# A hybrid RWKV backbone on one core: the RWKV stage, its group norms, the conditioning and the filters put in an order by a list scheduler for all five engines, and the triangular inverse made by 16-blocks on GpSimd

## The chip, the cores and the metric

The kernel runs on one core of a Trainium2 chip. The metric is the device time of one execution in microseconds (us); the kernel before was timed three times. Engines are named as in the profile: PE is TensorE (PEld its weight loads), DVE VectorE, ACT ScalarE, POOL GpSimd, SP SyncE, which here issues the DMA transfers and computes nothing.

## The reference

Two layers over 1024 latent and 256 context tokens of width 1024, in fp32. Layer 0 has retention and RWKV-7 side by side, layer 1 a Hyena long convolution and neighbourhood attention. The change touches RWKV (8 heads of 64, both directions), its group norm and bonus, the conditioning, and the Hyena filters:

```python
shift, scale, gate = jnp.split(sc @ ada_w[i] + ada_b[i], 3, axis=-1)   # sc = silu(c); the same with silu(c_ctx)
...
for d in range(2):
    w_log = -jax.nn.softplus(-(w0[d] + jnp.tanh(wd[:, :, d]) @ w2[d])) - 0.5
    a = jax.nn.sigmoid(a0[d] + ad[:, :, d] @ a2[d])
...
def step(s, inp):                                    # rwkv7_scan, one token
    r_t, w_t, k_t, v_t, kk_t, a_t = inp
    sa = jnp.einsum('bhvk,bhk->bhv', s, -kk_t)
    s = s * w_t[:, :, None, :] + sa[..., None] * (kk_t * a_t)[:, :, None, :] + v_t[..., None] * k_t[:, :, None, :]
    return s, jnp.einsum('bhvk,bhk->bhv', s, r_t)
...
gn = ((rw_y - mean) * lax.rsqrt(var + RWKV_GN_EPS)).reshape(bl, l, RWKV_W) * rw_ln_w + rw_ln_b
bonus = sum(jnp.sum(r * dirs[d][1] * rw_rk, axis=-1, keepdims=True) * v for d in range(2))
rw_o = (gn + bonus.reshape(bl, l, RWKV_W)) * jax.nn.silu(u[..., E_WZ:E_SHIFT])
...
hid = jnp.sin(f2 * (jnp.sin(f1 * (z @ w1 + b1)) @ w2 + b2))             # hyena_filters
h = (hid @ w3).reshape(length, HY_ORDER, 2, HY_W)
```

## The kernel before

The program runs in phases. Phase A makes layer 0's projections and the retention; its last projection product starts on PE at 673 us, and the rest of the retention follows. Phase B, which the change rewrites, is the RWKV stage with all that runs beside it. Phase C multiplies by layer 0's output weights; the later phases are layer 1.

RWKV is computed in chunks of 64 tokens, two chunks to a group, ten groups, both directions d side by side on the two halves of the 128 partitions. For each group and direction, `half` handles two head pairs at a time: loads `kkr`; the low-rank products `lora` on PE and four tanh `tw` on ACT; a running sum `cum` on DVE; decays `Pt`, `Pi` on ACT; scaled keys `AR`, `BK` on DVE and POOL; their transposes `BT`. `stage1` then makes the scores `sc` on PE, which DVE takes out of PSUM under a mask in two parts: `Ga` (key against key, to be inverted) and `Gr` (read-out). `inverse` inverts I minus 32 strictly triangular 64x64 matrices per group. It writes their diagonal 32-blocks to DRAM (`la`), loads them back with one matrix row to a free index (`AL`), does 31 steps of a multiply (L956) and an add (L958) on DVE, and goes back through DRAM (`lt`, `TT`). `merge` makes the off-diagonal block out of three rounds of 32x32 products on PE (`t11p`, `xp`, `t21p`), each copied out by ACT and DVE. `recur` walks the two chunks: read-out `rp` (from the state `SP`, with `Ga` and later `Gr`), `up` (the inverse times the right-hand side `RH`), the state update `sp`, and the result `Yg`, which goes to DRAM as `y`.

Beside it run three other pieces of work. `ada_gate` and `ada_cols` make the rest of the conditioning in 32 blocks of 128 columns, each a load of 512 KB (`aw`) and eight products (`adaps`) whose stationary side is only 2 columns wide. `RwkvOut.block` makes norm, bonus and gate for 128 tokens at a time, 10 blocks, as soon as both directions have them. `hyena_kernels` makes the filters (`hkps`, `HK`, `EO`, `d1ps`, `d2t`, `d2ps`), begun in the last groups and finished in phase C. The order on each engine comes from the tile framework, which schedules what the program emits; recurrence and group preparation are emitted under `tc.high_priority`, the side work by `next(side)` between the steps of `phase_b`.

## Time and profile before

| | before |
|---|---|
| median of 3 runs | 2403.91 us (2401.15 to 2409.35) |
| the profiled execution | 2408.1 us, span 2406.3 us |
| mean granted TensorE clock | 0.941 of full speed |
| PE busy in the span | 2206.3 us (92%) |
| DVE, ACT, POOL busy | 1213.9, 930.2, 791.6 us |
| instructions | 44212 |

Read it so: the share of 92% is an average over phases with different limits. What counts for this change are the rows from 680 to 1400 us, where PE is less busy and its granted clock lower than elsewhere.

### The profile page before, as it was taken

The page shows a single profiled execution, that of the slowest core. Times are in us where ns is not written, and L with a number is a line of the kernel's source. Part 1 is how long each engine was busy: PE and PEld are TensorE (multiplying, and loading weights), DVE is VectorE, ACT ScalarE, POOL GpSimd, SP SyncE. Part 2 cuts the span into 40 slices and gives each one's busy share as a digit, 9 for nine tenths or more (in the row PEclk, how much of TensorE's full clock was granted, in tenths as well). Part 3 has the DMA queues.
Part 4 walks back from the last instruction along what each step waited for, and adds up shares of the span by engine and source line. Part 5 has one row for each costly group of instructions (what it writes and reads, how often), then busy time and mean ns, then how long its engine had stood idle before and what let it go on. Part 6 is the DMA issues. An engine that isn't in the chain of part 4 may idle for free. (4 is left out here: it accounts for less than half of the span.)

```text
span 2406.3 us, 44212 instructions
## 1 busy us (share of the span) xinstructions
PE 2206.3 (92%) x16800; PEld 1854.7 (77%) x16800; DVE 1213.9 (50%) x3043; ACT 930.2 (39%) x1996; POOL 791.6 (33%) x1040
## 2 busy tenths in 40 slices
PE   7999999999989788898868899999979999989997
PEld 3778878777856677777766689889968888878987
DVE  6301222234347687777777756610036666634438
ACT  4321124445345354444335543321124444444432
POOL 2313625453556243333214534521111011010133
PEclk9999999999988787788889999999989999999999
DMA  7323333544276544455455443433276462175453
GB/s 245 95 78 106 116 115 123 155 126 136 91 211 180 119 124 126 108 134 138 101 145 170 151 160 107 148 115 109 75 184 162 130 169 93 53 242 156 132 161 123
DMA packets 398365, 325.66 MB, mean 135 GB/s; under 512 B 135038, under 2 KB 337928, under 8 KB 397898
## 3 DMA queue, kind: packets, MB, share of 16 engines
q1 hardware_dynamic: 398154, 322.85, 46.5%
q8 instruction: 133, 2.18, 0.4%
q14 instruction: 78, 0.64, 0.1%
HBM read 227.58 MB, written 95.17 MB: 134 GB/s over the span
## 5 line engine op out<-in xcount | busy, mean ns | idle before, releaser
L386 POOL TENSOR_TENSOR wlo<-wraw,whi 128x512 fp32r<-128x512 f32 (+1 forms) x60 | 81.6, 1380 | 354.7 <-ACT whi L385 303.0
L418 PE MATMUL dps<-n1hi,whi 128*128 128x512 f32 x448 | 187.5, 418 | 0.1
L418 PE MATMUL dps<-n1hi,wlo 128*128 128x512 f32 x448 | 177.4, 396 | 0.0
L418 PE MATMUL dps<-n1lo,whi 128*128 128x512 f32 x448 | 177.1, 395 | 0.0
L418 PE MATMUL dnp<-wlo,nhi 128*128 128x512 f32 x400 | 159.1, 399 | 2.9 <-POOL wlo L402 2.9
L418 PE MATMUL dnp<-whi,nlo 128*128 128x512 f32 x400 | 158.3, 397 | 0.0
L418 PE MATMUL dnp<-whi,nhi 128*128 128x512 f32 x400 | 153.3, 399 | 1.6 <-ACT whi L401 1.6
L402 POOL TENSOR_TENSOR wlo<-wraw,whi 128x512 fp32r<-128x512 f32 (+1 forms) x72 | 92.3, 1291 | 131.4 <-ACT whi L401 126.5
L418 PE MATMUL mmps<-nhi,whi 128*128 128x512 f32 (+1 forms) x336 | 123.4, 368 | 2.9 <-ACT vto L533 2.1
L327 PE MATMUL adaps<-aw,sc 128*2 128x128 f32 (+1 forms) x640 | 114.2, 335 | 11.6 <-DMA aw<-in_ada_w 9.6
L418 PE MATMUL mmps<-nlo,whi 128*128 128x512 f32 (+1 forms) x336 | 120.8, 361 | 0.0
L418 PE MATMUL mmps<-nhi,wlo 128*128 128x512 f32 (+1 forms) x336 | 119.6, 365 | 0.0
L956 DVE TENSOR_TENSOR tm<-RR,AL 128x126 f32<-128x126 f32 (+22 forms) x310 | 99.7, 322 | 19.5 <-DMA AL<-la 13.3
L1254 POOL TENSOR_TENSOR hn<-hn,xr 128x256 f32<-128x256 f32 x60 | 47.2, 791 | 175.4 <-DVE hn L1253 158.8
L418 PEld LDWEIGHTS dps<-n1hi,wlo 128*128 128x128 f32 x448 | 85.1, 190 | 18.6
L327 PEld LDWEIGHTS adaps<-aw,sc 128*2 128x2 f32 x640 | 55.3, 94 | 56.4 <-issue 16.7
L958 DVE TENSOR_TENSOR RR<-RR,tm 128x126 f32<-128x126 f32 (+22 forms) x310 | 94.6, 305 | 6.2
L418 PE MATMUL ops<-whi,clo 128*128 128x256 f32 x320 | 89.7, 287 | 6.1 <-DVE clo L1187 6.1
L418 PEld LDWEIGHTS dps<-n1hi,whi 128*128 128x128 f32 x448 | 85.9, 192 | 11.0 <-ACT whi L385 0.6
L418 PEld LDWEIGHTS dps<-n1lo,whi 128*128 128x128 f32 x448 | 85.6, 191 | 10.5
L418 PE MATMUL ops<-whi,chi 128*128 128x256 f32 x320 | 92.8, 292 | 0.0
L418 PEld LDWEIGHTS dnp<-wlo,nhi 128*128 128x128 f32 x400 | 75.7, 189 | 22.0 <-POOL wlo L402 4.7
(400 smaller groups left out, 6188.9 us busy)
## 6 DMA issues: line engine op xcount, KB each, us to landing
aw<-in_ada_w SPq DMA_DIRECT2D x32, 512.0 KB
kkr<-kkr SPq DMA_DIRECT2D x40, 384.0 KB
wraw<-in_odd_w_in SPq DMA_DIRECT2D x56, 256.0 KB
wraw<-in_even_w_in SPq DMA_DIRECT2D x48, 256.0 KB
bi<-in_nab SPq DMA_DIRECT2D x64, 192.0 KB
aw<-in_ada_w SPq DMA_DIRECT2D x8, 1024.0 KB
spec<-KS SPq DMA_DIRECT2D x32, 256.0 KB
h<-hn SPq DMA_DIRECT2D x16, 512.0 KB
```

What stands on the lines that cost most here:

```text
L327: nc.tensor.matmul(ps[0:2, :n], self.sc[:, k, :], w[:, k, :], start=k == 0, stop=k == 7)
L386: (lo_eng or nc.gpsimd).tensor_tensor(lo[:, kk:kk + 4], raw, hi[:, kk:kk + 4].bitcast(F32), op=ALU.subtract)
L402: nc.gpsimd.tensor_tensor(lo[:, :n], raw[:, :n], hi[:, :n].bitcast(F32), op=ALU.subtract)
L418: nc.tensor.matmul(ps, a, b, start=start and n == 0, stop=stop and n == 3 * nk - 1)
L956: nc.vector.tensor_tensor(t3, RR[:, 0:n, q:q + 1].to_broadcast([P, n, w]), AL[:, q:q + 1, q + 1:32].to_broadcast([P, n, w]), op=ALU.mult)
L958: nc.vector.tensor_tensor(RR[:, 0:n, q + 1:32], RR[:, 0:n, q + 1:32], t3, op=ALU.add)
L1254: add.tensor_tensor(h[:, cs], h[:, cs], x[:, cs], op=ALU.add)
```

## The change

`Sched` is a list scheduler that runs while the kernel is being built. Each piece of work is a generator that yields an engine and an assumed cost ahead of each instruction or run of instructions, `wait` for named results and `get` for a buffer, with a rank; `Sched.run` takes, for the engine that comes free first, the startable request with the lowest rank, and so writes the order of all five engines, SP's transfers among them. The whole of phase B is emitted so under `tc.manual_schedule`. Ranks: the recurrence 0, merges 0.5, inverse 1, value loads 1.5, group preparation 2, then the side work.

Along with the order, these things change. The inverse goes by 16-blocks: 15 steps on POOL of at most 64 elements to a partition in place of 31 on DVE of up to 136, through three DRAM buffers `la`, `ld`, `lt` whose matrices have a pitch of 65 and whose diagonal blocks are read in pieces of 64 B. The merge becomes four rounds of two halves, each half 16 products of 64x64 and one DVE instruction of 128x512. `Ga` and `Gr` become one tile `G`, taken out of PSUM in one 128x512 instruction for each half. `lora` is issued with the directions alternating, into two PSUM tiles; `sp` with column halves alternating; the read-out products with `G` with d alternating; the first read-out uses 64 rows instead of 128. The conditioning's stationary side is padded to 32 columns and its eight products go to four column groups of 32, added up afterwards by a product with `sel`. Memsets of `Pt`, `UV` and `RH` go away.

```diff
+class Sched:
+    HOP, LOOK = 0.12, 0.15
...
+            first = {}
+            for _, e, _, at, *_ in self.ready:
+                first[e] = min(first.get(e, 1e9), max(self.free.get(e, 0.0), at))
+            e = min(first, key=first.get)
+            r = min((r for r in self.ready if r[1] == e and r[3] <= first[e] + self.LOOK * (e != "")), key=lambda r: r[0])
...
-            nc.tensor.matmul(ps[0:2, :n], self.sc[:, k, :], w[:, k, :], start=k == 0, stop=k == 7)
+            g = 32 * (k % 4)
+            nc.tensor.matmul(ps[g:g + 32, :n], self.sc[:, k, :], w[:, k, :], start=k < 4, stop=k > 3)
...
+    def lora(self, g, hp):
...
+        t = yield "PE", 1.8
+        pss = [self.b1([P, 2, 2, P], "lora") for _ in range(2)]
+        for j, w in enumerate((self.w2, self.a2)):
+            for q, d in itertools.product(range(2), range(2)):
+                p = 2 * hp + q
+                nc.tensor.matmul(pss[d][:, j, q, :], w[HALF[d], p * P:(p + 1) * P], wa[HALF[d], j, :], start=True, stop=True)
...
+            t = yield "DVE", 0.7
+            nc.vector.tensor_tensor(G[:, h].rearrange("p t q c -> p q t c"), ps.rearrange("p (q t) c -> p q t c", q=2),
+                                    m[:, None, None, :].to_broadcast([P, 2, 2, P]), op=ALU.mult)
...
-        for q in range(31):
...
+        nc.sync.dma_start(AL, self.blocks("la", g))
+        t += 2.6
+        for q in range(15):
+            t = yield "POOL", 0.66, t
...
+            nc.gpsimd.tensor_tensor(t3, RR[:, 0:n, q:q + 1].to_broadcast([P, n, w]),
+                                    AL[:, q:q + 1, q + 1:16].to_broadcast([P, n, w]), op=ALU.mult)
+            nc.gpsimd.tensor_tensor(RR[:, 0:n, q + 1:16], RR[:, 0:n, q + 1:16], t3, op=ALU.add)
...
+        for n, src in (("ld", RR), ("lt", RT)):
+            t = yield "SP", 0.1
+            nc.sync.dma_start(self.blocks(n, g), src)
+            ts.append(t + 2.4)
...
+        for j in range(4):
+            for hp in range(2):
...
+                yield "PE", 0.8
+                ps = self.pc.tile([P, 8, C], F32, name="mg", tag="mg", bufs=1)
...
+                t = yield "DVE", 0.7
...
+            for p, d, h in itertools.product(range(4), range(2), range(2)):
+                nc.tensor.matmul(sp[HALF[h], p, d, :], half("bt", d, p)[:, (p % 2) * NS + t, h * C:h * C + C], uh(d, p, h),
+                                 start=True, stop=True)
...
+        def over():
+            n = 4 * rw.NG - 4
+            t = yield ("wait", *((k, n + j) for j in range(4) for k in ("prod", "G", "bt", "pc")))
+            sch.mark("over", t)
...
+        Filters(s, D, sch, opened).start("over")
+        E = mybir.EngineType
+        with tc.manual_schedule(engines={E.PE, E.DVE, E.Activation, E.Pool, E.SP}):
+            sch.run()
```

Three places show how the order moves. The first is the inverse of one group. Before, on DVE, late in one such run (L956 multiplies, L958 adds, L923 and L925 take scores out of PSUM):

```order
L956 TENSOR_TENSOR tm<-RR,AL 128x91
L958 TENSOR_TENSOR RR<-RR,tm 128x13x7
L956 TENSOR_TENSOR tm<-RR,AL 128x78
L958 TENSOR_TENSOR RR<-RR,tm 128x13x6
L956 TENSOR_TENSOR tm<-RR,AL 128x70
L958 TENSOR_TENSOR RR<-RR,tm 128x14x5
L956 TENSOR_TENSOR tm<-RR,AL 128x56
L958 TENSOR_TENSOR RR<-RR,tm 128x14x4
L923 TENSOR_TENSOR Ga<-sc,cst 128x256
L925 TENSOR_TENSOR Gr<-sc,cst 128x256
```

After, on POOL, at its beginning (L1036 to L1043 make the next keys; L1141 and L1143 are the steps):

```order
L1036 TENSOR_TENSOR km<-km,kkr 128x256
L1041 TENSOR_TENSOR BK<-tw,Pi 128x4x64
L1004 TENSOR_TENSOR AR<-kkr,Pt_6106 128x4x64
L1043 TENSOR_TENSOR BK<-km,Pi 128x4x64
L1141 TENSOR_TENSOR tm<-RR,AL 128x15
L1143 TENSOR_TENSOR RR<-RR,tm 128x15
L1141 TENSOR_TENSOR tm<-RR,AL 128x28
L1143 TENSOR_TENSOR RR<-RR,tm 128x2x14
L1141 TENSOR_TENSOR tm<-RR,AL 128x39
L1143 TENSOR_TENSOR RR<-RR,tm 128x3x13
L1141 TENSOR_TENSOR tm<-RR,AL 128x48
L1143 TENSOR_TENSOR RR<-RR,tm 128x4x12
```

The steps have left DVE's row; on POOL they stand one behind the other, after the key products that were ready before them.

The second is PE's row where the retention ends and RWKV begins (qp, rsp, ryp, rbs belong to the retention). Before:

```order
L774 MATMUL rbs<-rn_3800,cst 128x512
L743 MATMUL qp<-cst,qk 128x128 x3
L752 MATMUL rsp<-qT 128x128 x2
L327 MATMUL adaps<-aw,sc 2x128 x8
L757 MATMUL ryp<-qD,SS 64x128
L758 MATMUL ryp<-sT,qk 64x128
L757 MATMUL ryp<-qD,SS 64x128
L758 MATMUL ryp<-sT,qk 64x128
L743 MATMUL qp<-cst,qk 128x128 x3
L327 MATMUL adaps<-aw,sc 2x128 x7
L857 MATMUL lora<-wa,w_6096 128x128 x2
L327 MATMUL adaps<-aw,sc 2x128
```

After:

```order
L806 MATMUL ryp<-qD,SS 64x128
L807 MATMUL ryp<-sT,qk 64x128
L801 MATMUL rsp<-qT 128x128 x2
L806 MATMUL ryp<-qD,SS 64x128
L807 MATMUL ryp<-sT,qk 64x128
L806 MATMUL ryp<-qD,SS 64x128
L807 MATMUL ryp<-sT,qk 64x128
L823 MATMUL rbs<-rn_3974,cst 128x256
L940 MATMUL lora<-wa,w_6093 128x128 x4
L940 MATMUL lora<-wa,a_6094 128x128 x4
L940 MATMUL lora<-wa,w_6093 128x128 x4
```

The retention's last products and the first `lora` stood among one another; now the whole retention stands ahead of the first `lora`, and the conditioning's products come behind it. ACT and DVE have the same cut.

The third is one merge on PE in the steady state. Before (three rounds of 32x32 products; the second and third round shown):

```order
L979 MATMUL xp<-TX,Ga 32x32 x14
L921 MATMUL sc<-AR,BK 128x128 x8
L857 MATMUL lora<-wa,a_6097 128x128 x2
L979 MATMUL t21p<-TT_6118,TY 32x32 x32
L891 MATMUL btp<-cst,BK 128x128 x4
L857 MATMUL lora<-wa,w_6096 128x128 x2
L891 MATMUL btp<-cst,BK 128x128 x4
L1002 MATMUL up<-RH,TT_6118 64x64 x16
L921 MATMUL sc<-AR,BK 128x128 x4
```

After (`mg` are the merge's halves):

```order
L1184 MATMUL mg<-lt,G 64x64 x16
L1413 MATMUL adaps<-aw,scw 32x128 x8
L1088 MATMUL btp<-cst,BK 128x128 x4
L1184 MATMUL mg<-lt,G 64x64 x16
L1423 MATMUL adat<-sel,adarow 128x2
L1068 MATMUL sc<-AR,BK 128x128 x4
L1184 MATMUL mg<-ld,HTt 64x64 x16
L1088 MATMUL btp<-cst,BK 128x128 x4
L1068 MATMUL sc<-AR,BK 128x128 x4
L1184 MATMUL mg<-ld,HTt 64x64 x16
L1068 MATMUL sc<-AR,BK 128x128 x4
L1184 MATMUL mg<-TT,HTt 64x64 x16
```

Each half of a round now has other work of the next group behind it, where a round had been one run of 32 products.

## Rows read from the trace of the kernel before

**Rows 1.** The page of before: the span, and the granted clock of PE in 40 equal slices (60.2 us each), in tenths.

```profile
span 2406.3 us, 44212 instructions
PEclk9999999999988787788889999999989999999999
```

**Rows 2.** Busy time in seven stretches of 50 us from 835 to 1185 us, of which two and the sum: the stretch, its length, then PE, PEld, DVE, ACT, POOL (busy us and instructions), the granted clock, the DMA share, GB/s; the last row is the sum with the means.

```profile
985.00:1035.00 50.00, 39.97 (x546) 32.76 (x545) 34.88 (x95) 18.68 (x44) 18.04 (x30) 0.77 0.54 128
1035.00:1085.00 50.00, 45.51 (x627) 37.85 (x626) 35.99 (x102) 22.60 (x54) 18.86 (x32) 0.89 0.55 141
...
sum 350.00, PE 302.72 PEld 261.04 DVE 269.04 ACT 151.63 POOL 128.08; mean PE 43.25 PEld 37.29 DVE 38.43 ACT 21.66 POOL 18.30
```

**Rows 3.** PE's groups of instructions from 835 to 1185 us: line, out<-in, shapes, records; then busy us, mean ns; then PE's idle time ahead of them and what ended it.

```profile
L327 PE MATMUL adaps<-aw,sc 128*2 128x128 f32 x285 | 43.7, 312 | 0.8 <-DVE mc L295 0.8
L1016 PE MATMUL rp<-UV,Gr 128*64 128x64 f32 x416 | 34.5, 247 | 0.3 <-ACT UV L1005 0.2
L1008 PE MATMUL sp<-UV,BT 128*64 128x64 f32 x416 | 27.3, 238 | 2.4 <-DVE UV L1005 2.4
L857 PE MATMUL lora<-wa,a 64*128 64x128 f32 x96 | 21.9, 362 | 10.1 <-ACT tw L861 10.1
L857 PE MATMUL lora<-wa,w 64*128 64x128 f32 x92 | 20.7, 356 | 0.0
L1002 PE MATMUL up<-RH,TT 128*64 128x64 f32 x448 | 20.4, 259 | 8.0 <-DVE RH L999 7.6 <-DVE TT L981 0.3
L996 PE MATMUL rp<-UV,Ga 128*64 128x64 f32 x416 | 15.0, 225 | 0.0
L979 PE MATMUL t11p<-cst,TT 128*32 128x32 f32 x448 | 12.2, 216 | 5.6 <-DMA TT<-lt 5.6
L979 PE MATMUL t21p<-TT,TY 32*32 32x32 f32 x448 | 11.2, 217 | 7.0 <-DVE TY L981 6.9
L979 PE MATMUL xp<-TX,Ga 32*32 32x32 f32 x448 | 10.7, 211 | 4.1 <-DVE TX L981 4.1
L293 PE MATMUL adat<-cst,adarow 2*128 2x2 f32 x20 | 4.6, 297 | 9.3 <-DVE adarow L290 9.3
```

**Rows 4.** Instructions that carry one tile, from 675 to 1300 us: number, minimum/median/maximum in ns, start of the first and of the last.

```profile
L1002 PE MATMUL up<-RH,TT x640: 222/222/369, 813.7 to 1287.4; 128*64 128x64 f32 x160
L861 ACT ACTIVATE tw<-lora,hc x160: 342/360/376, 693.6 to 1150.4; 128x128 f32<-128x128 f32 x160
```

**Rows 5.** Timeline of PE from 672 to 745 us: start, length, line, out<-in, [idle before it, and what ended that].

```profile
673.00 0.49 PE L743 MATMUL qp<-cst,qk 128*128 128x128 f32 x3
...
676.18 0.52 PE L743 MATMUL qp<-cst,qk 128*128 128x128 f32 x3 [0.53 <-DMA qk<-rqkv]
...
683.72 0.87 PE L743 MATMUL qp<-cst,qk 128*128 128x128 f32 x3
...
692.76 0.71 PE L857 MATMUL lora<-wa,w 64*128 64x128 f32 x4
...
693.71 0.49 PE L752 MATMUL rsp<-qT 64*128 64x128 f32 x4
...
722.69 0.55 PE L743 MATMUL qp<-cst,qk 128*128 128x128 f32 x3
```

**Rows 6.** Timeline of the first group's inverse and merge: SP's issues, DVE and PE.

```profile
733.50 1.03 SPq L946 DMA_DIRECT2D la<-Ga  x2
742.21 0.42 DVE L956 TENSOR_TENSOR tm<-RR,AL 128x31 f32<-128x31 f32 x1 [0.79 <-DMA AL<-la]
787.68 1.31 SPq L960 DMA_DIRECT2D lt<-RR  x2
802.34 1.21 PE L979 MATMUL t11p<-cst,TT 128*32 128x32 f32 x64
813.75 1.98 PE L1002 MATMUL up<-RH,TT 128*64 128x64 f32 x32 [0.94 <-DVE TT L981]
```

**Rows 7.** POOL's and DVE's groups by form, 675 to 1436 us (the second row is of the whole span: minimum/median/maximum).

```profile
L888 POOL COPY PCt<-Pt 128x4 f32<-128x4 f32 x40 | 9.9, 259 | 5.7 <-ACT Pt L870 3.4 <-DVE S L1011 1.4 <-DVE tm L956 0.9
L735 POOL TENSOR_TENSOR SS<-SS,st x72: 447/454/462, 245.3 to 670.9; 64x128 f32<-64x128 f32 x72
L956 DVE TENSOR_TENSOR tm<-RR,AL 128x30 f32<-128x30 f32 x20 | 4.3, 213 | 0.4
L958 DVE TENSOR_TENSOR RR<-RR,tm 128x30 f32<-128x30 f32 x20 | 4.6, 228 | 0.5
L923 DVE TENSOR_TENSOR Ga<-sc,cst 128x256 f32<-128x256 f32 x80 | 33.5, 418 | 11.3 <-PE sc L921 10.6
L1327 DVE TENSOR_TENSOR HK<-hkps,win 128x512 f32<-128x512 f32 x32 | 22.0, 686 | 11.6 <-PE hkps L1325 6.7 <-POOL EO L1332 4.7
```

**Rows 8.** The two groups of the inverse on the page.

```profile
L956 DVE TENSOR_TENSOR tm<-RR,AL 128x126 f32<-128x126 f32 (+22 forms) x310 | 99.7, 322 | 19.5 <-DMA AL<-la 13.3
L958 DVE TENSOR_TENSOR RR<-RR,tm 128x126 f32<-128x126 f32 (+22 forms) x310 | 94.6, 305 | 6.2
```

**Rows 9.** The first eviction of the output product of layer 0: minimum/median/maximum in ns, first and last start.

```profile
L1196 DVE TENSOR_TENSOR hn<-ops,gb x40: 410/425/426, 1399.4 to 1540.6; 128x256 f32<-128x256 f32 x40
```

**Rows 10.** DMA from 835 to 1185 us: packets, bytes, and how many packets are small.

```profile
DMA packets 89893, 44.07 MB, mean 126 GB/s; under 512 B 42589, under 2 KB 82849, under 8 KB 89843
```

**Rows 11.** The waits from 835 to 1185 us: engine, line, what it waited for: us in total, times, longest.

```profile
POOL UV L931 <- PE sp L1008: 68.7, 11, 14.2
```

More of the change, by code (lines that the diff above doesn't have):

```diff
@@ new lines, in __init__, with start @@
+        nc.sync.dma_start(self.eye.rearrange("p a b -> p (a b)"), i["eyel"])
+        Z = pl.tile([P, 1040], F32, name="Z", tag="HT", bufs=1)
+        nc.gpsimd.memset(Z, 0.0)
+        for n in ("ld", "lt"):
+            for j in range(2):
+                nc.sync.dma_start(D[n][j].rearrange("d (a n) -> (d a) n", n=1040), Z)
+        self.T = {}
+    def start(self):
+        add, ALL = self.sch.add, range(self.NG)
+        for g in ALL:
+            add(2 + g / 100, self.wa(g))
+            for hp in range(2):
+                add(2 + g / 100 + hp / 1000, self.lora(g, hp))
+            for n in range(4 * g, 4 * g + 4):
+                r = 2 + g / 100 + n % 4 / 2000
+                for f in (self.load, self.chain, self.keys, self.scores, self.turn, self.end):
+                    add(r, f(n))
+            for t in range(self.NS):
+                add(1.5, self.values(g, t))
+            add(1 + g / 100, self.inverse(g))
+            add(0.5, self.merge(g))
+        add(0, self.recur())
@@ L862, in half, with chain @@
-        th, ta = tw[:, 0], tw[:, 1]
+        return [nat(L[:, :, j, :]) for j in range(3)], v4, u4
+    def chain(self, n):
+        nc, sch, T, pf, C = self.s.nc, self.sch, self.T, self.pf, self.C
+        g, d, hp = self.split(n)
+        ca, cr = (0, 64) if d == 0 else (64, 0)
+        yield "wait", ("tw", n), ("kkr", n)
+        yield "get", "tmp"
+        (kt, kkt, rt), v4, u4 = self.views(n)
+        th = T["tw", n][:, 0]
+        t = yield "ACT", 0.43
+        sch.mark(("tmp", n), t)
         nc.scalar.activation(th, th, AF.Copy, scale=0.5, bias=0.5)
-        cum = pf.tile([P, 2, P], F32, name="cum", tag="cum", bufs=1)
+        yield "DVE", 0.87
+        cum = pf.tile([P, 2, P], F32, name="cum", tag="cum", bufs=2)
@@ L997, in recur @@
                                  skip_group_check=True)
+            if t:
+                for _ in range(4):
+                    sch.put("ar", e)
             for d in range(2):
-                copy[d](RH[HALF[d], d], rp[d][HALF[d]])
+                yield copy[d][1], copy[d][2], e
+                if d == 0:
+                    RH = pl.tile([P, 4, 2, C], F32, name="RH", tag="RH", bufs=1)
+                copy[d][0](RH[HALF[d]], rp[d][HALF[d]])
+            e = yield "PE", 1.1
             up = pc.tile([P, 4, 2, C], F32, name="up", tag="c2")
```

971 lines of the change are left out of this document (626 added, 345 removed).

## The prediction

> **What bounds the kernel now.** I read the page first. The granted clock stands at 0.9 or more of full speed in all slices but 10 to 20, about 600 to 1260 us [rows 1]; that is the RWKV stage, and the only part the change rewrites. So I looked at its steady state in stretches of 50 us. The twenty chunk steps are counted by `up` on PE: the first at 813.7 us, the last at 1287.4 [rows 4], 19 intervals, or 473.7 / 19 x 2 = 49.9 us a group. The 350 us from 835 to 1185 are therefore seven groups, and the sums there divide by seven: PE busy 43.25 us a group, DVE 38.4, ACT 21.7, POOL 18.3 [rows 2]. PE is the bound, busy 87% of the time at a clock between 0.77 and 0.89, a mix of its two levels, 1.2 and 2.4 GHz; DVE stands close behind. Then PE's groups of instructions, busy time beside the idle time ahead of each: of the idle 47.3 us (350 less 302.7) most end on DVE (adat 9.3, up 7.6, t21p 6.9, xp 4.1, sp 2.4), ten on ACT's tanh at `lora`, 5.6 on a transfer [rows 3]. So there are three gains to look for: fewer PE us, less idle time, an earlier start.
>
> **PE's busy time, over seven groups.** The price of overlap comes from two rows alike in shape and count: 416 records of 128x64 take 15.0 us as `Ga` products, issued with the output halves alternating, and 34.5 as `Gr` products, issued one half after the other [rows 3].
> (a) `Gr` with d alternating: 34.5 to 15.0, -19.5.
> (b) `sp` with column halves alternating: 27.3 to about 15, -12.
> (c) `lora` with the two row halves alternating: a burst of four on one row half takes 0.71 us, the retention's `rsp`, four on two halves, 0.49 [rows 5]; less a start-up that both hold, I put that at half, 42.6 to 21, -21.
> (d) `adaps` in four column groups: 43.7 to about 22, -22, if two at a time overlap, as in the pair above. The bounds are no overlap (0) and four at a time (11, -33).
> (e) Merge: 12.2 + 11.2 + 10.7 = 34.1 go. Eight halves of 16 products are 128 products a group; `up` has 32 a group and 64 records, so 256 records, at the 45.5 ns of `up` (20.4 / 448, also 64 rows into alternating halves) 11.65 us a group, 81.6 in seven: +47.5.
> Sum: -19.5 - 12 - 21 - 22 + 47.5 = -27, or -3.9 a group: 39.4 us.
>
> The Trainium skill, "TensorEngine Tiling (Array Packing)", Theoretical Speedup, says that with 32 columns up to four products run at once. By that (d) would be 11 instead of 22, another 1.6 us a group, an estimate of 2301 in place of 2316; no row of before has such a form.
>
> **PE's idle time** is 6.75 us a group. DVE loses the inverse, (99.7 + 94.6) / 10 = 19.4 us a group [rows 8], and the merge copies (3 x 0.69), and gains eight merge instructions of 128x512 at 0.69 (as L1327), 5.5; the scores' evictions stay about equal, 8 of 0.69 for 16 of 0.42 [rows 7]. That is 38.4 - 19.4 - 2.1 + 5.5 - 1.2, about 21 us. With DVE half as full I halve the waits that end on it (36 to 18 in seven groups) and half of lora's (a second PSUM tile lets PE run ahead). What remains is 47 - 18 - 5, some 24, plus a transfer that comes late now and then, 5: 4.2 a group. Bounds: nothing gained (6.75) and 1. The new period is 39.4 + 4.2, about 43.5, and the gain 6.4 over the 9.5 groups between the first and the last step: **-61**. With the bounds on idle it lies between -36 and -90.
>
> POOL takes the inverse. Its row of before has nothing so small in its stage; the nearest are a copy of 128x4 at 0.26 and the retention's 64x128 sum at 0.45 [rows 7]. For 30 instructions of at most 64 elements I take 0.30 and a little between them: 10 us, bounds 7.5 and 13.5. POOL goes from 18.3 a group to about 27 (the `UV` memsets leave it), well under the period. Transfers: by the code the small packets a group about double, since 16-blocks are read in 64 B pieces; now they are 42589 in seven groups at a DMA share of about 0.5 [rows 2, 10]. I cost that at nothing, covered by the key work of the next group; uncovered it is the second rival.
>
> **The start.** Now `lora` starts at 692.8, between the retention's pairs [rows 5]; in the new order it stands behind all of them, on PE, ACT and DVE alike. From 683.72 on there are six pairs (qp from 683.72 to 722.69) and two norms. A pair alone takes 3.18 us (673.00 to 676.18); the next qp came 7.54 later, so a norm costs 4.3 more. The first tanh moves from 693.6 to 683.7 + 12.8 + 4.3 + 6.4 + 4.3 + 1.3, about 713. From there to the last `la` of the first group took 40 us (693.6 to 733.5) among retention work; without it I put 27 (bounds 18, POOL's own busy time a group, and 40): 740. Then, as in the first group now: 8.7 to the first step of the inverse, on POOL 10 us where DVE needed 45.5 (742.2 to 787.7, its work of the next group between), 14.6 from `lt` to the merge (787.7 to 802.3) [rows 6], and 13 for the merge (8 halves of about 0.8 on PE and 0.7 on DVE, partly overlapped, where it took 11.4). First `up` at 787 instead of 813.7: **-27**, bounds -9 and -40.
>
> The Trainium skill, "GPSIMD Engine Reference", Key points, says that elementwise work is about twice as fast on DVE. By that the 30 instructions cost twice DVE's 0.21 and 0.23 for 30 elements, an estimate of 13 us and not 10, which gives back some 4 us here (2320); nothing in the steady state, where POOL has room.
>
> **The end.** From the last `up`, 1287.4, to phase C's first eviction, 1399.4 [rows 4, 9], are 112 us of remaining filters, norms and weight loads. In the orders about as many filter products stand ahead of phase C as before, and the norms of the last blocks still follow the last steps. I take 112 again; what follows is untouched.
>
> **Sum.** 2408.1 (the profiled execution) - 61 - 27 = 2320. It stands 4.2 over the median of 2403.9, so the time to expect of a timing is **2316**; this case's own range is 2270 to 2360, the bounds of idle time and start.
>
> **Rivals.**
> (1) The clock rises. It lies at 0.83 between the two stretches shown and at 0.9 and more outside the stage [rows 1, 2]. If the denser row holds it near 1, PE's 39.4 us shrink to 0.83 x 39.4, about 33; with 4 of idle that is 36.9, a gain of 13 x 9.5 = 124 and 27: about 2253. For it: PE's idle time falls. Against: the products that now overlap in pairs leave PE less to do, and the share stays about 90%.
> (2) The order is made with transfers of 2.3 to 2.8 us, where `la` to the first step took 8.7 and `lt` to the merge 14.6 with two transfers in it [rows 6]. If merge products stand in PE's row where the plan has their data and the chip has not, PE stops. At 5.5 us a group less 2 that other waits give way the period is 47: -28 - 27, about 2349.
> (3) Slower than before: queues that stand. POOL's inverse waits for `AL` in order, and the next keys stand behind it; PE's merge waits for `ld`, `lt`, with recurrence products behind it. Even now POOL's UV memset stood 68.7 us behind PE's sp products [rows 11], without harm, as nothing urgent was behind it. If both round trips lie open in each group, 9.2 us of uncovered wait (6.4 + 27 / 9.5) use up the whole gain; at 12 us the period is 55.5 and the time about 2430.
> (4) The period does not change at all because the recurrence's own chain sets it, and the start's gain is lost to the retention: no change.
>
> **Chances.** My forecast 0.48, (1) 0.23, (2) 0.11, (3) 0.13, (4) 0.05. Over 0.3%, about 7 us, is what a measurement of this kernel can tell from no change. Faster is 0.48 + 0.23 + 0.11 = 0.82, the same 0.05, slower 0.13. The range reaches from below (1) to just under no change: 2235 to 2400, and leaves out most of (3) and the edges.
>
> **What would show it.** Right: some 43 to 44 us between every second `up` start, PE busy 39 to 40 a group with `adaps`, `lora`, Gr and sp at about half, merge near 11.7; the first `up` near 787 with the first tanh near 713; POOL's steps near 0.3 us; about 112 us from the last `up` to the first eviction. Wrong: PE waits of more than 5 us at the merge for `ld` or `lt`; POOL waits for `AL` with late keys behind them; a granted clock of 0.95 in the stage; adaps no cheaper; or a longer stretch behind the last step, with filters and norms that the shorter recurrence no longer covers.

## The result, and the profile after

The changed kernel takes 2422.04 us in the median of 5 runs (2417.6 to 2430.56), before beside it on the same chip 2401.15 (2400.52 to 2409.35): a ratio of 1.0086, 95% interval 1.0057 to 1.0114. It is slower by 0.9%. Its profiled execution took 2428.3 us with a span of 2426.3.

The page of after, span and PE's granted clock in 40 slices of 60.7 us (the answer to [rows 1]):

```profile
span 2426.3 us, 45045 instructions
PEclk9999999999955978799888999999989999999999
```

The stage's clock is about what it was, but for two slices at 0.5 between 667 and 788 us, which are new. The tiles that mark the start, the steps and the end (answers to [rows 4, 9]; number, minimum/median/maximum in ns, first and last start):

```profile
L949 ACT ACTIVATE tw<-lora,hc x160: 344/368/412, 727.5 to 1186.3; 128x128 f32<-128x128 f32 x160
L1237 PE MATMUL up<-RH,TT x640: 218/218/363, 808.9 to 1303.8; 64*64 64x64 f32 x160
L1697 DVE TENSOR_TENSOR hn<-ops,gb x40: 409/423/426, 1424.9 to 1566.3; 128x256 f32<-128x256 f32 x40
```

The first `up` comes 4.8 us earlier, not 27. The nineteen intervals take 494.9 us instead of 473.7: 52.1 us a group, not 43.5. From the last `up` to phase C it is 121.1 us instead of 112.0. What follows is 5.5 shorter. The sum, -4.8 + 21.2 + 9.1 - 5.5, is the 20.0 by which the span grew. Seen from PE over the whole span (a line of after's page), it is busy 53.5 us less than the 2206.3 of before, and idle 273.5 us where it was 200.0, so the saved work is there and more than lost in waiting:

```profile
PE 2152.8 (89%) x17472; PEld 1829.0 (75%) x17472; DVE 1070.0 (44%) x2411; ACT 913.8 (38%) x1976; POOL 858.5 (35%) x1271
```

Seven stretches of 52 us, seven groups, of which two and the sum (columns as in [rows 2]):

```profile
850.00:902.00 52.00, 39.30 (x580) 34.73 (x580) 19.86 (x36) 15.93 (x36) 24.47 (x55) 0.73 0.66 150
1058.00:1110.00 52.00, 38.97 (x694) 34.22 (x694) 23.55 (x43) 19.26 (x44) 23.05 (x53) 0.90 0.73 145
...
sum 364.00, PE 289.50 PEld 254.76 DVE 184.91 ACT 146.63 POOL 184.29; mean PE 41.36 PEld 36.40 DVE 26.42 ACT 20.95 POOL 26.33
```

PE has less to do than before (41.4 us a group for 43.25), DVE 12 us less. No engine is busy for more than 80% of the period. PE is idle 10.6 us a group where it was 6.75. Its groups in these 364 us (columns as in [rows 3]; two groups that interleave both count the time that they share, so the groups add up to more than 289.5):

```profile
L1068 PE MATMUL sc<-AR,BK 64*128 64x128 f32 x421 | 67.0, 308 | 4.8 <-POOL BK L1043 4.8
L1184 PE MATMUL mg<-TT,HTt 64*64 64x64 f32 x800 | 30.3, 229 | 2.2 <-DVE TT L1193 2.2
L1184 PE MATMUL mg<-lt,G 64*64 64x64 f32 x414 | 27.0, 300 | 50.1 <-DMA lt<-lt 50.1
L1237 PE MATMUL up<-RH,TT 64*64 64x64 f32 x448 | 17.3, 227 | 4.0 <-ACT RH L1232 2.2 <-DVE RH L1232 1.7
L1184 PE MATMUL mg<-ld,HTt 64*64 64x64 f32 x384 | 16.7, 248 | 0.0
L1247 PE MATMUL sp<-UV,BT 128*64 128x64 f32 x448 | 16.7, 229 | 6.8 <-DVE UV L1243 6.8
L1413 PE MATMUL adaps<-aw,scw 128*32 128x128 f32 x336 | 16.6, 326 | 0.0
L1269 PE MATMUL rp<-UV,G 128*64 128x64 f32 x448 | 16.1, 227 | 0.0
L940 PE MATMUL lora<-wa,w 64*128 64x128 f32 x104 | 11.0, 320 | 0.0
L940 PE MATMUL lora<-wa,a 64*128 64x128 f32 x104 | 9.6, 294 | 0.0
```

Of the idle 74.5 us two thirds, 50.1, stand ahead of the merge's first products, for the transfer of `lt`: 7.2 us in each group. The product waits are otherwise nearly gone: lora's 10.1, `up`'s 8.0 and adat's 9.3 of [rows 3] are 0, 4.0 and 1.6.

One such wait. SP's row, from the last `la` of a group to its merge blocks, the first products that need them on PE, and POOL's inverse (start, length, line, out<-in):

```profile
909.15 0.61 SPq L1075 DMA_DIRECT2D la<-G  x1
911.78 0.37 SPq L1133 DMA_DIRECT2D AL<-la  x1
...
928.15 0.37 SPq L1151 DMA_DIRECT2D ld<-RR  x1
928.80 0.63 SPq L1151 DMA_DIRECT2D lt<-RT  x1
929.48 3.06 SPq L921 DMA_DIRECT2D wa<-wa  x2
932.64 1.30 SPq L1160 DMA_DIRECT2D ld<-ld  x2
934.04 1.89 SPq L1160 DMA_DIRECT2D lt<-lt  x2
```

```profile
915.51 0.21 POOL L1141 TENSOR_TENSOR tm<-RR,AL 128x15 f32<-128x15 f32 x1
...
916.10 0.23 POOL L1141 TENSOR_TENSOR tm<-RR,AL 128x28 f32<-128x28 f32 x1
...
922.36 0.84 POOL L1141 TENSOR_TENSOR tm<-RR,AL 128x63 f32<-128x63 f32 x1
...
927.89 0.23 POOL L1143 TENSOR_TENSOR RR<-RR,tm 128x15 f32<-128x15 f32 x1
```

```profile
934.78 1.10 PE L1269 MATMUL rp<-UV,G 128*64 128x64 f32 x32
939.69 0.47 PE L1184 MATMUL mg<-lt,G 64*64 64x64 f32 x2 [3.81 <-DMA lt<-lt]
942.63 1.97 PE L1184 MATMUL mg<-lt,G 64*64 64x64 f32 x30 [2.46 <-DMA lt<-lt]
944.52 3.09 PE L1068 MATMUL sc<-AR,BK 64*128 64x128 f32 x16
```

From the last `la` to the first merge product it is 30.5 us: 2.6 until SP may issue `AL`, 3.7 to POOL's first step, 12.6 for the thirty steps, then 6 from the first write to the last block load, with the `wa` loads between them, and 5.7 from the issue of the last `lt`. PE's row has the merge at a place where the scheduler's table has `lt` in SBUF; its figures for these stages (2.5, 2.6, 9.9, 0.45, 2.4, 2.5) add up to 20.4. Behind the waiting product stand the scores of the next group, `sc` at 944.52, which need nothing of it (POOL's last key product for them ended at 934.9).

### The profile page after: what moved, and what is told of

It is laid out like the page before. It is cut to its first block, busy times and chain, and to the rows that moved or that the text cites. A ratio compares the mean times of both kernels' runs of the same rounds, so it can differ in the third digit from the quotient of the medians.

```text
span 2426.3 us, 45045 instructions
## 1 busy us (share of the span) xinstructions
PE 2152.8 (89%) x17472; PEld 1829.0 (75%) x17472; DVE 1070.0 (44%) x2411; ACT 913.8 (38%) x1976; POOL 858.5 (35%) x1271
## 5 line engine op out<-in xcount | busy, mean ns | idle before, releaser
L435 POOL TENSOR_TENSOR wlo<-wraw,whi 128x512 fp32r<-128x512 f32 (+1 forms) x60 | 81.6, 1381 | 358.6 <-ACT whi L434 288.8
L1068 PE MATMUL sc<-AR,BK 64*128 64x128 f32 x640 | 104.5, 315 | 13.0 <-POOL BK L1043 12.8
L1068 PEld LDWEIGHTS sc<-AR,BK 64*128 64x128 f32 x640 | 88.2, 214 | 25.1 <-POOL BK L1043 14.9
L1184 PE MATMUL mg<-lt,G 64*64 64x64 f32 x640 | 40.0, 292 | 64.9 <-DMA lt<-lt 64.9
L467 PEld LDWEIGHTS dps<-n1lo,whi 128*128 128x128 f32 x448 | 85.3, 190 | 10.3
L467 PE MATMUL ops<-whi,chi 128*128 128x256 f32 x320 | 91.5, 288 | 0.4 <-ACT whi L434 0.4
L467 PE MATMUL ops<-wlo,chi 128*128 128x256 f32 x320 | 90.8, 285 | 1.0 <-POOL wlo L435 1.0
L467 PEld LDWEIGHTS dnp<-wlo,nhi 128*128 128x128 f32 x400 | 75.5, 189 | 19.2 <-POOL wlo L451 2.1
```

The source lines that it names most:

```text
L435: (lo_eng or nc.gpsimd).tensor_tensor(lo[:, kk:kk + 4], raw, hi[:, kk:kk + 4].bitcast(F32), op=ALU.subtract)
L467: nc.tensor.matmul(ps, a, b, start=start and n == 0, stop=stop and n == 3 * nk - 1)
L1068: nc.tensor.matmul(ps[:, u, :], T["bk", n][HALF[h], u, :], T["ar", n][HALF[h], u, :], start=True, stop=True)
L1184: nc.tensor.matmul(ps[HALF[d], u, :], lh, rh, start=True, stop=True)
```

## The experiments

Theories. **Work (P):** PE is the bound as forecast, and the added products (scores, merge) make the period. **Loop (L):** the trip through DRAM, the inverse and back is longer than the table has it, so PE stands at `mg`. **Rows (R):** the fixed rows of several engines stand at several places, and shortening one stage moves the wait to the next row. The fourteen experiments beside before and after, with the start of the first `up`, the length from first to last `up` ("steps", 9.5 periods), and from there to the first eviction of phase C (profiled execution, us):

| kernel | median (before beside it) | ratio [95%] | first `up` | steps | to phase C |
|---|---|---|---|---|---|
| before | 2401.15 | | 813.7 | 473.7 | 112.0 |
| after | 2422.04 (2401.15) | 1.0086 [1.0057, 1.0114] | 808.9 | 494.9 | 121.1 |
| e1 half the inverse, after | 2418.91 (2407.07) | 1.0042 [1.0002, 1.0082] | 811.7 | 484.1 | 123.2 |
| e2 ada twice, after | 2434.84 (2407.07) | 1.0089 [1.0038, 1.014] | 816.6 | 493.3 | 122.2 |
| e3 ada quarter, before | 2431.03 (2407.07) | 1.0065 [1.0025, 1.0104] | 829.8 | 489.2 | 107.3 |
| e4 half the inverse, before | 2364.17 (2407.07) | 0.9774 [0.9714, 0.9835] | 789.6 | 423.2 | 149.0 |
| e5 real transfers | 2400.24 (2406.89) | 0.9969 [0.9953, 0.9986] | 818.1 | 466.5 | 100.9 |
| e6 real transfers and PE | 2403.45 (2406.89) | 0.9971 [0.9945, 0.9997] | 817.6 | 475.1 | 108.9 |
| e7 start on ACT's queue | 2425.64 (2406.89) | 1.0073 [1.0058, 1.0088] | 811.4 | 505.6 | 99.4 |
| e8 inverse alone, POOL | 2427.9 (2406.35) | 1.009 [1.0058, 1.0121] | 835.1 | 486.5 | 87.2 |
| e9 inverse alone, DVE | 2427.08 (2406.35) | 1.0085 [1.0053, 1.0117] | 816.4 | 494.0 | 108.9 |
| e10 ada twice, before | 2452.2 (2406.35) | 1.0181 [1.0139, 1.0223] | 819.2 | 462.5 | 166.1 |
| e11 e5 with scores paired | 2380.36 (2403.23) | 0.9886 [0.9843, 0.9928] | 811.4 | 461.5 | 91.5 |
| e12 e11 with the start | 2357.02 (2403.23) | 0.9805 [0.976, 0.9851] | 795.9 | 445.8 | 105.5 |
| e13 half the inverse, e12 | 2355.89 (2406.7) | 0.9784 [0.972, 0.9849] | 793.0 | 444.2 | 107.3 |
| e14 ada twice, e12 | 2361.5 (2406.7) | 0.981 [0.9754, 0.9866] | 800.5 | 452.3 | 107.2 |

The part behind phase C's first eviction, which no edit touches, takes 996 to 1016 us in these profiles, and the steps of e7, whose edit touches only the start, are 10.7 us longer than after's. So differences of some 10 us between two profiles in one column are not told from chance.

**Is it PE's work?** e2 does the conditioning products of after twice (the second pass starts the sums anew).

```diff
-        for k in range(8):
+        for k in (*range(8), *range(8)):
```

> The changed kernel with the eight conditioning products of each block in the RWKV stage issued twice (the gates and the modulation come out doubled); the order is otherwise unchanged. They take 17.0 us of PE in seven groups now, so PE gets 2.4 us a group more. Theory L (the period is the loop through la, the inverse and lt): the added work lies in PE's waits, where it stands ahead of the merge, and the period rises by 1 us or less, 0 to 10 us in all. Theory P (PE's own work sets it): +2.4 us a group, 23 us in all or more, about 2445.

Measured: 704 `adaps` records take 27.6 us in the 364 us in which 336 took 16.6, 1.6 us a group more. PE's busy time rises by some 1 us a group, as the granted clock of the stretch is 0.88 for 0.84, and the steps do not get longer (493.3 for 494.9); PE's wait for `lt` shrinks instead:

```profile
L1413 PE MATMUL adaps<-aw,scw 128*32 128x128 f32 x704 | 27.6, 306 | 0.0
L1184 PE MATMUL mg<-lt,G 64*64 64x64 f32 x384 | 23.4, 288 | 40.5 <-DMA lt<-lt 40.5
```

Of the 10.3 us by which its span is longer than after's, 7.7 lie ahead of the first `up`; its ratio, 1.0089, is no other than after's 1.0086. By these rows PE's work does not set the period of after. But some 10 us in all is little to add, beside what one profile can tell; e11 below asks it with four times as much, the other way round. The same is asked of before by e10 (twice) and e3 (only two of the eight products).

> The kernel before with the eight conditioning products of each block in the RWKV stage issued twice (the second pass starts its sums anew, so the results stay). They take 43.7 us of PE in seven groups, so PE gets 6.2 us a group more. Theory P (PE's work sets the period): +6 us a group, about 60 us, 2460. Theory C (PE has slack, and its granted clock rises as it is kept busy): the mean clock from 835 to 1185 us rises above 0.9 and the time stays within 15 us of before, to either side.

```diff
-        for k in range(8):
+        for k in range(8) if n > P else (0, 7):
```

> The kernel before with six of the eight conditioning products of each block in the RWKV stage left out. They take 43.7 us of PE in seven groups, so PE gets 4.7 us a group less. Theory P (PE bounds the RWKV stage of the kernel before, as the prediction put it): the period falls from 49.9 to about 45.5 and the kernel by some 42 us, to about 2360. Theory L (a chain through the inverse bounds it there too): the period stays within 1 us and the kernel within 10 us.

Measured: e10 loses 46 us. That is nearer to P (60) than to C (at most 15, with a clock over 0.9; it is 0.84 from 835 to 1185 us). Its steps are shorter (462.5), but few of the added products stand there: 370 `adaps` records in the 350 us of [rows 3], not twice 285. The loss lies behind the steps, 166.1 for 112.0: the filters, which follow the conditioning in the emitted order, begin at 1272.9 instead of 1257.0, and 254 instead of 176 of the `d1ps` records lie between the last `up` and phase C's first eviction. PE's line of e10's page:

```profile
PE 2243.7 (92%) x17312; PEld 1875.0 (77%) x17312; DVE 1213.4 (50%) x3043; ACT 931.7 (38%) x1996; POOL 791.2 (32%) x1040
```

PE is busy 37.4 us more than the 2206.3 of before and idle 207.1 us where it was 200.0, so most of the 44.5 us by which the span grew is PE's own added time. In before, where the framework places the side work (here the filters moved), work on PE does cost time; this agrees with "PE is the bound" there. e3, with less work, is slower than before, by 24 us, but it takes no time off PE: over the span PE is busy 2211.9 us, as the products that are left ran at a lower clock (last section). So e3 does not settle the question.

**Is it the table's figures?** e5 puts the trace's durations into the scheduler for the transfers, SP's issues, the copy `RT` and the inverse's steps (some of the lines shown); e6 those of PE's bursts too, with the other loads at 4.0 us where e5 has 3.5.

```diff
-        sch.mark(("la", n), t + 2.5)
+        sch.mark(("la", n), t + 2.8)
...
-        t += 2.6
+        t += 3.7
-            t = yield "POOL", 0.66, t
+            t = yield "POOL", 0.77, t
...
-            ts.append(t + 2.4)
+            ts.append(t + 3.6)
...
-        sch.mark(("dd", g), t + 2.5)
+        sch.mark(("dd", g), t + 5.0)
```

> The changed kernel with the scheduler's assumed times for the inverse's way set to what its own trace shows: la 2.8 us, AL to the first step 3.7, a pair of steps 0.77, the copy RT 0.65, the writes of ld and lt 3.6, their loads 5.0, the other loads 3.5, an issue on SP 0.3. Nothing but the order changes. Theory O (the order was made for transfers that are too short, so that PE, ACT and SP stand in their fixed rows): PE's wait at the merge falls from 7.2 us a group to 2 or less, the period from 52.1 to 46 or 47, the time by 45 us or more, to about 2370. Theory Q (any fixed order of that kind has a loop as long, since merge and scores share PE's row): the wait goes elsewhere, the period stays above 50 and the time within 10 us of 2422.

```diff
-                yield "PE", 0.8
+                yield "PE", 1.2
...
-        e = yield "PE", 1.9
+        e = yield "PE", 1.2
```

> As the run with real transfer times, and PE's assumed costs set to the trace as well: a burst of scores 1.2 for 1.0, the read-out with the state 2.0 for 1.0, a half of a merge round 1.2 for 0.8, lora 1.4 for 1.8, the read-out behind the step 1.2 for 1.9. Theory O: at least as good as with real transfers alone, period 45 to 47, about 2365. Theory Q: as there, within 10 us of 2422.

Measured: e5 gives back all of the loss, 22 us against after's median, with no other work and no other instruction, by the order alone: the steps fall from 494.9 to 466.5. PE's wait for `lt` in 363 us:

```profile
L1184 PE MATMUL mg<-lt,G 64*64 64x64 f32 x448 | 27.9, 296 | 29.5 <-DMA lt<-lt 28.6 <-DVE HTt L1189 0.9
```

28.6 for 50.1. That is half of what theory O expected (2 us or less a group, 45 us in all): 3.9 us a group stay. Which of the figures did it was not tried one by one. In e6 it is 14.4, and yet the period is no shorter than e5's (50.0 for 49.1). PE's busy time in 364 us is 312.9 there, 43.0 a group for after's 41.4, and 7.0 of idle time a group are left. Less waiting at this place is not a shorter period by as much.

**Is it the length of the inverse?** Every second step is left out, in after by e1 and in e12 (a later kernel, below) by e13, with the order kept, and in before by e4, with `range(0, 31, 2)`. The edit of e1 and e13:

```diff
+            if q % 2:
+                t -= sch.HOP
+                continue
```

> The changed kernel with every second of the inverse's 15 steps left out (so the inverse is not one); the order on all engines is unchanged. In the changed kernel the steps take 11.5 us on POOL from the first to the last, PE stands 7.2 us a group at the merge's first products for lt, and a group takes 52.1 us. Theory L (the period is a loop in a fixed order: last scores, la, AL, inverse, lt, merge, and behind the merge the next scores): the steps get 5.5 us shorter, the wait at the merge falls to about 2 us a group and the period to about 47; some 50 us less in all, about 2372. Theory P (PE's own work sets the period, the wait is only an effect): no change, 2422.

> The kernel before with every second of the inverse's 31 steps left out (so the inverse is not one); DVE gets some 9.4 us a group less and the first inverse, 45 us long, some 20 us shorter. Theory P (PE bounds the stage): the first up comes about 20 us earlier, the period falls by no more than the DVE waits, 1 to 2 us; 30 to 40 us less in all. Theory L (the chain through the inverse sets the period): the period falls by 5 us or more, 70 us or more in all, under 2335.

> The run with paired scores and the other start (period 46.9 us, PE busy 37.5 of it), with every second of the inverse's 15 steps left out (so the inverse is not one) and the order unchanged. Theory L (the loop la, AL, inverse, lt, merge, next scores sets the period): 5.5 us shorter steps, the period falls by 3 us or more, 30 to 50 us in all, under 2330. Theory R (each engine's row stands at several places of about equal length, so that taking one away only shows the next): the period falls by less than 2 us and the time by less than 20, as it was in the changed kernel itself. Theory P (PE's work): no change.

Measured: in after the inverse falls to 5.9 us, yet the wait at `mg` stays (51.0 in seven groups), and the period falls by 1.1 us only, not by the 5 that Loop asks. In e13 nothing moves beyond the noise. What takes the inverse's place is seen on ACT and SP of e13, where the inverse of this group ended at 889.06:

```profile
892.62 1.26 ACT L1273 COPY SP<-S 64x512 f32<-64x512 f32 x2 [0.63 <-DVE S L1267]
893.90 1.18 ACT L1293 COPY Yg<-rp 64x512 f32<-64x512 f32 x2
895.11 0.62 ACT L1158 COPY RT<-RR 128x256 f32<-128x256 f32 x1
```

```profile
894.50 1.21 SPq L1299 DMA_DIRECT2D y<-Yg  x2
...
896.49 0.57 SPq L1162 DMA_DIRECT2D ld<-RR  x1
897.16 3.49 SPq L1162 DMA_DIRECT2D lt<-RT  x1
```

`RR` was ready 6 us before the copy, but its transposing copy `RT` stands on ACT behind the state and result copies of the step before, and the writes of `ld` and `lt` on SP behind the result `y` of that step. So the writes leave behind that step's results, however early the inverse ended: from the issue of `AL` to the write of `lt` it is 16.6 us in e13 and 16.8 in e12 (means of the ten groups, from the starts in SP's timelines), though the inverse took 5.7 us in e13 and 11.2 in e12. That is Rows, not Loop, as far as these rows show; no run gave `RT` another place.

In before, where the framework orders and the steps sit on DVE among all else, half of them was worth 43 us (two timings): the steps shrink from 473.7 to 423.2 as under L, but 37 us come back between the last `up` and phase C, where the side work went. Of the 48.3 us that its span is shorter, PE's busy time makes 35.9 with the same products, at a clock of 0.89 in the steps where before has 0.81. How much is the chain and how much the clock stays open.

**The start.** PE and SP of after, behind the retention's last product:

```profile
703.57 1.22 PE L823 MATMUL rbs<-rn,cst 128*128 128x256 f32 x2 [0.86 <-ACT rn L821]
724.03 0.79 PE L940 MATMUL lora<-wa,w 64*128 64x128 f32 x2 [19.23 <-DMA wa<-wa]
```

```profile
708.43 0.32 SPq L827 DMA_DIRECT2D cat<-rn  x1
...
711.62 1.00 SPq L886 DMA_DIRECT2D ld<-Z  x2
712.66 2.35 SPq L886 DMA_DIRECT2D lt<-Z  x2
715.30 2.90 SPq L1112 DMA_DIRECT2D UV<-vt  x3
718.25 0.60 SPq L921 DMA_DIRECT2D wa<-wa  x1
```

The first `wa` is issued 10 us after the retention's last store `cat`, behind zero fills and values that nobody needs yet. PE stands for 19.2 us. The granted clock is low in this stretch as well: 0.50 from 700 to 725 us, which is the lower of the two levels, with PE busy 4.7 us of the 25, and 0.55 from 725 to 750, where before has 0.93 and 0.91. e7 moves `wa` of group 0 and the first three `kkr` to ACT's queue.

```diff
+        q, eng = ("ACT", nc.scalar) if g == 0 else ("SP", nc.sync)
         for d in range(2):
-            t = yield "SP", 0.1
+            t = yield q, 0.1
...
-            nc.sync.dma_start(wa[HALF[d]], D["wa"][HALF[d], :, t0:t0 + P])
+            eng.dma_start(wa[HALF[d]], D["wa"][HALF[d], :, t0:t0 + P])
```

> The changed kernel with the first group's wa load and the first three kkr loads issued from ACT's queue instead of SP's, where wa stood behind 14 transfers and PE waited 19.2 us for it. With that the retention's end and the first preparation stand among one another again on PE and ACT. If SP's row is what cost the start: the first tanh comes at about 695 to 705 us instead of 727.5 and the first up at about 785 instead of 809; the steps behind are as before, so about 20 us less, 2400. If the first inverse waits for something else: the first up stays above 800 and the time within 8 us of 2422.

Measured: the first tanh comes at 686.3 instead of 727.5, and the first `up` at 811.4 all the same; the clock is 0.50 from 700 to 750 us here too. The wait went one product on, to the conditioning's load, still on SP's row behind `cat`:

```profile
730.97 1.08 PE L1415 MATMUL adaps<-aw,scw 128*32 128x128 f32 x16 [20.24 <-DMA aw<-in_ada_w]
```

e12 takes this one away too: it lets conditioning start behind the first group's `la`, puts the zero fills on POOL's queue and the first values behind `kkr` (and each later load of values behind the `up` copy before it). It keeps e7's edit, and also holds **the scores**, which e11 tries alone on top of e5: the two row halves alternate, into two PSUM tiles.

```diff
-            for u in range(4):
-                nc.tensor.matmul(ps[:, u, :], T["bk", n][HALF[h], u, :], ...)
+        for u in range(4):
+            for h in range(2):
+                nc.tensor.matmul(pss[h][:, u, :], T["bk", n][HALF[h], u, :], ...)
```

```diff
-                nc.sync.dma_start(D[n][j].rearrange("d (a n) -> (d a) n", n=1040), Z)
+                nc.gpsimd.dma_start(D[n][j].rearrange("d (a n) -> (d a) n", n=1040), Z)
...
+        yield "wait", ("uv", g - 1 + t, 1 - t) if g + t else ("kkr", 2)
...
-        if n:
-            yield "wait", ("ada", n - 1)
+        yield "wait", ("ada", n - 1) if n else ("la", 3)
```

> The run with real transfer times, and one more edit: the score products of the two row halves are issued alternating, as lora is, into two PSUM tiles taken together. In the changed kernel they take 67.0 us of PE in seven groups, 9.6 a group; alternating should make that about 5. PE was busy 42 of 49 us a group in the run with real transfer times. If PE's work now sets the period: 49.1 to about 45, 35 to 40 us less than that run, about 2362. If the loop through the inverse or the granted clock sets it: the period stays above 48 and the time within 10 us of 2400.

> The run with paired scores and a start of another order: wa and the first three kkr loads on ACT's queue, the four fills of ld and lt on POOL's, the value loads behind the kkr loads, and the conditioning held back until the first group's la is out. In the run with the start on ACT's queue alone the first tanh came at 686 us, but PE then stood 20.2 us at a conditioning product for its aw load and the first up still came at 811. If that wait was what was left of the start: the first up at about 780 to 785 and 25 us or more less than the run with paired scores alone. If the first up stays at 800 or above: something else holds the first group, and the gain is under 10 us.

Measured, the scores' row of e11 in 329 us:

```profile
L1072 PE MATMUL sc<-AR,BK 64*128 64x128 f32 x432 | 36.5, 314 | 0.6 <-DVE mc L1431 0.6
```

In after 421 records took 67.0 us. PE's busy time falls from 41.8 us a group in e5 to 37.7, and the period hardly answers (48.6 for e5's 49.1); of the 21 us by which the span is shorter than e5's, 7 lie ahead of the first `up`, 5 in the steps, and 9 behind the last. e12 brings the first `up` to 795.9, 13 us ahead of after, with the first tanh at 683.1, and the period to 46.9. At 2357.02 us, a ratio of 0.9805 (0.976 to 0.9851), it is faster than before and after. Its first `up` lies between the two forecasts (780 to 785, or 800 and above): PE now stands 15.2 us for POOL's keys ahead of the first scores, and its clock is 0.50 from 700 to 725 us as in after. That wait, and the row of the merge's first products in 300 us of the steps:

```profile
722.34 2.08 PE L1074 MATMUL sc<-AR,BK 64*128 64x128 f32 x16 [15.23 <-POOL BK L1047]
```

```profile
L1192 PE MATMUL mg<-lt,G 64*64 64x64 f32 x384 | 23.7, 293 | 30.8 <-DMA lt<-lt 28.1 <-DVE HTt L1197 2.8
```

The wait at `mg` is still 4.4 us a group. e14 asks e2's question again, of e12.

> The run with paired scores and the other start, with the eight conditioning products of each block in the RWKV stage issued twice (the second pass starts its sums anew, so the results stay), the order otherwise unchanged: PE gets some 2.2 us a group more. Theory P: the period rises by 2 us or more, 20 us or more in all. Theories L and R: it lies in PE's waits, the period rises by less than 1 us and the time by less than 10.

Measured: the period rises by 0.7 us, as under L and R, for 1.5 us of added products a group (27.3 us of `adaps` in 300 for 17.6). But PE's busy time is 37.6 us a group as in e12 (37.5), since the clock of the stretch is 0.93 for 0.90 and the other products took less. So e14 added no time on PE, and for e12 the question is not settled by it; that PE is idle there for 9 us of 47 is what the rows show.

**The inverse alone.** e8 puts only the 16-block inverse and the four-round merge into before, in the framework's order, the steps on POOL; e9 has them on DVE.

```diff
-        for q in range(31):
-            n, w = q // 2 + 1, 31 - q
+        for q in range(15):
+            n, w = q + 1, 15 - q
...
-            nc.vector.tensor_tensor(RR[:, 0:n, q + 1:32], RR[:, 0:n, q + 1:32], t3, op=ALU.add)
+            nc.gpsimd.tensor_tensor(RR[:, 0:n, q + 1:16], RR[:, 0:n, q + 1:16], t3, op=ALU.add)
```

> The kernel before with one part of the change alone: the inverse by 16-blocks on POOL, its three DRAM buffers and the merge in four rounds of two halves; the order stays the framework's, Ga and Gr, lora, sp and the conditioning stay as they were. Theory O (the inverse by 16-blocks is a gain, and the hand-made order loses it): DVE gets some 16 us a group less, the first up comes before 795, the period falls to about 45 as with half the steps left out, and the time is about 2360. Theory I (the inverse's new way itself is the loss: small pieces through DRAM, and a merge of 11 us on PE instead of 5): period 52 or more, the time 2415 or more.

> As the run with the 16-block inverse in the kernel before, with the 15 steps on DVE instead of POOL: about 7 us of DVE a group. If POOL's in-order row (keys of the next group, waiting memsets) holds the steps up, DVE is better by 10 us or more; if not, the two are within 8 us of each other.

Measured: both lose 21 us. The steps take 486.5 and 494.0 us instead of 473.7. Which engine has the steps makes no difference that can be told (ratios 1.009 and 1.0085). DVE has 11 us a group less in e8 than before, and nothing comes of it; PE has more (seven stretches from 860 us on):

```profile
sum 350.00, PE 313.67 PEld 271.78 DVE 189.60 ACT 142.53 POOL 191.69; mean PE 44.81 PEld 38.83 DVE 27.09 ACT 20.36 POOL 27.38
```

44.8 us in 50, at a period of 51.2 some 45.9 a group, where before had 43.25. Over the whole span PE is busy 21.8 us more than in before and idle 5.5 less, so the loss is PE's added time, as in e10. This part of the change is a loss by itself in before's order; whether it is one in the new order was not tried. What paid in the runs is the order with real figures (e5), and the paired scores and the other start on top of it (e11, e12).

## Why the prediction was wrong

Forecast 2320 for the profiled execution, measured 2428.3: 108 us. Of these the period is (52.1 - 43.5) x 9.5 = 82, the first `up` 22, the end 9, what follows -5.5. In the period, PE's busy time is 2.0 us a group over the forecast and its idle time 6.4: 19 and 61 of the 82.

**PE's busy time: sizes near, the sum short by what it left out.** In seven groups `Gr` 16.1 (forecast 15), `sp` 16.7 (15), `lora` 20.6 (21), merge 74.0 (81.6) and `adaps` 16.6 (22). The Trainium skill, "TensorEngine Tiling (Array Packing)", Theoretical Speedup, had up to four at once for (d). 49 ns a record in place of 153 [rows 3] is a gain of 3.1, so the row lies between my pair and the page. Not in the sum were the scores, whose bursts the new code splits by row half, 67.0 us for 55.9 in before's same 350 us, and the read-out from the state (32.8 for 26.8) and the conditioning's transposes (8.9 for 4.6). PE came to 41.4 us a group and not 39.4.

**PE's idle time: the failed step.** I took the 6.75 us of before, halved what ended on DVE, and left "a transfer that comes late now and then, 5" in seven groups. The waits on DVE did fall, further than I said: 12.6 us in seven groups end on it (forecast 18). The transfer's were 50.1 us in seven groups, ten times my figure. The mistake was to make an idle term by subtraction from the old order, when the new order was written out and its assumed figures could be laid beside the trace: 20.4 us from `la` to the merge in the code, where [rows 6] show 8.7 us from `la` to the first step and 14.6 from `lt` to the merge for what the code has as 5.1 and 4.9. In after the second of these is 9.6 to 14.1 in the ten groups. I had that as rival (2), with 5.5 us a group at 11%, and it was 7.2. e5 shows the cause for about half of it: with the trace's figures the wait is 3.9. For the rest the rows of ACT and SP (e13) are the likely cause, which is argued and not shown.

**The step ahead of it, "PE is the bound", was carried over without a reason.** In before, e10 agrees with it. In after PE's row is fixed and PE is idle 10.6 us of 52.1: e2's added work ends in the wait for `lt`, and e11 takes 4 us a group off PE for 0.5 us of period. So a saving on PE was no longer a saving of time.

**Rival (3)** is where it ended, slower, though not by POOL standing behind `AL`: that wait is 11.2 us in 364, 1.6 a group. The other half, PE behind `lt`, came with the start and the end. Its 2430 is near the measured time by luck: it has a period of 55.5 and a start that gains 27 us.

**Rivals (1) and (4):** the seven clocks of the stage have a mean of 0.84 where before has 0.81, a little of (1), and nothing came of it (before's seven go from 0.71 to 0.89; the 0.77 and 0.83 of the prediction are those of the two stretches shown); the period did change, so (4) is out.

**The start:** forecast 787, measured 808.9. The retention was off PE at 704.8, earlier than I worked out; the first tanh came at 727.5 (forecast 713), as SP's row has `wa` behind `cat` and twelve more issues. I counted PE, ACT and DVE rows there and not SP's. From the tanh to the merge it went faster than I had it: the first merge product stands at 781.3, 8 us late. The other 14 us are the merge, 27.6 us for my 13. PE was not waiting in it:

```profile
781.00:809.00 28.00, 25.96 (x426) 22.75 (x428) 13.47 (x24) 11.73 (x34) 12.27 (x26) 0.86 0.57 140
```

Scores, `lora`, transposes and conditioning of the next groups stand between its halves, and I had put only its own products there. What the low clock from 667 to 788 us cost is not known. **The end:** 121 for 112; no run says why.

**Right:** POOL at 26.3 us a group (27); its inverse took 11.0 to 12.6 us (10, bounds 7.5 to 13.5); small packets doubled (89369 in 364 us for the 42589 of [rows 10]), at a price that no run takes apart, since the transfers that PE waits for are among them. DVE is at 26.4 us a group, not 21, which cost nothing that the rows show. The Trainium skill, "GPSIMD Engine Reference", Key points, has POOL at half of DVE's pace; POOL's step of 128x28 takes 0.23 us and DVE's of 128x30 0.21 [rows 7], so at this size the trace does not show that factor; the 13 us that I drew from it are near the 12.6 for another reason, the larger steps of 0.3 to 0.8 us and some 0.1 between any two.

## What to carry to other kernels

Where a kernel writes its own order, take the assumed figures out of its code and lay each beside the trace first: a fixed row stood whole here at a figure that was too short, and correcting the figures was worth as much here as the whole change lost. An engine busy 87% of the time may be the bound in one order and not in the next; repeat some of its work once, see if the time moves, and read from the rows whether its busy time really rose (in e14 it did not). In a row of issues, count what stands ahead of the first load that anyone waits for, on SP's queue as on the engines.

## What was not expected of the hardware

Less work on PE went with a lower granted clock. One of seven stretches of e3 (columns as in [rows 2]), and their sum:

```profile
885.00:935.00 50.00, 36.74 (x459) 31.96 (x457) 44.02 (x119) 25.78 (x66) 20.14 (x33) 0.67 0.52 138
...
sum 350.00, PE 285.72 PEld 252.31 DVE 263.82 ACT 150.48 POOL 126.09; mean PE 40.82 PEld 36.04 DVE 37.69 ACT 21.50 POOL 18.01
```

The seven clocks have a mean of 0.77 where before has 0.81, with PE busy 40.8 us in 50 for 43.25. The 30 us of `adaps` that were left out gave back 17 only; the state update took 35.7 us for about as many products as before's 27.3 (419 records, 416):

```profile
L1008 PE MATMUL sp<-UV,BT 128*64 128x64 f32 x419 | 35.7, 279 | 3.0 <-DVE UV L1005 3.0
```

The other way round, the runs with added products have a higher clock in the steps: e2 0.88 for after's 0.84, e10 0.84 for before's 0.81, e14 0.93 for e12's 0.90. In these runs the clock so gave back part of what was added to PE or taken from it, and an experiment of that kind has to be read with the clock beside it. The order of the busy shares is not that of the clocks: e8 is busy 44.8 us in 50 at a mean of 0.92, e4 44.6 at 0.89, e12 only 40 at 0.86 to 0.97. e3 also has another order by the framework, so how much of its 24 us is the clock and how much the order stays open.
